# A two-layer diffusion trunk on one core: thirteen inverse square roots, from a VectorE iteration to one GpSimd power each

## The chip, the cores and the metric

The kernel runs on one core of one Trainium2 chip. The metric is the device time of one launch in microseconds (us). Engines are named as the profile names them: PE (TensorE matmuls), PEld (its weight loads), DVE (VectorE), ACT (ScalarE), POOL (GpSimd), SP (SyncE, which issues most DMAs). Each engine works through its own instruction list strictly in order and waits on semaphores for the others.

## The reference, cut to what matters

The reference is one inference step of a trunk of two layers over 384 tokens of width 1024 (128 context tokens and 256 latent tokens). Each layer has an adaLN-modulated RMSNorm, four token mixers that all read the same normed input (A: grouped-query attention, B: gated linear attention, C: differential attention, D: latent attention), gates, an output projection, a second modulated RMSNorm and a gated MLP with a width-3 convolution. One RMSNorm ends the program. What the change touches is the inverse square root in every RMSNorm:

```python
def rmsnorm(x, g):
    xf = x.astype(jnp.float32)
    y = xf * lax.rsqrt(jnp.mean(xf * xf, axis=-1, keepdims=True) + EPS)
    return (y * g.astype(jnp.float32)).astype(x.dtype)

# trunk_layer, twice
h = rmsnorm(x, p['norm1_g']) * (1.0 + sc1) + sh1      # width 1024
aq = rmsnorm(z['a_q'].reshape(...), p['a_qnorm_g'])   # per head, width 64; ak likewise
dq = rmsnorm(z['d_q'], p['d_qnorm_g']) @ p['d_w_uq']  # width 192; d_kv likewise, 128
ob = rmsnorm(ob_raw, p['b_onorm_g']) * silu(...)      # per head, width 64
oc = rmsnorm(oc_raw, p['c_onorm_g']) * (1.0 - lam_init)
h = rmsnorm(x, p['norm2_g']) * (1.0 + sc2) + sh2      # width 1024
```

## The kernel before, in words

Activations for the big projections lie feature-major, in eight tiles of 128 features by 384 tokens. Every fp32 product is made of three fast matmuls: each operand is split into a high and a low part (`wh`, `wl` for weights, `hh`, `hl` for the normed input), and PE does high by high, high by low and low by high. So each weight tile that SP loads (`raw`) passes ACT (a cast to `wh`) and DVE (`wl = raw - wh`) before PE can use it. Matmuls into PSUM banks named `d` are these projections; banks `m` serve the mixers, `x` the sums and broadcasts.

No order is written out by hand. All work is written as streams (Python generators) that yield one instruction, or a short list, at a time. A planner keeps a modelled clock for each engine and always emits next the instruction that could start earliest, then by priority. The order of every engine's list is thus an outcome of the planner's prices. An instruction other than a matmul or a DMA is priced by `price`, and its result counts as ready after the engine's latency in `LAT`, with 130 ns for an engine that `LAT` doesn't list (GpSimd):

```python
LAT = dict(zip("PVS", LATS))                 # LATS = (210.0, 130.0, 210.0)
...
if self.eng == "S":
    return (51 if psum else 93) + 93 * cols + 0.833 * n
...
return (129 if cols and self.fn in ("scalar_tensor_tensor", "tensor_scalar") else 68) + n * (0.521 if fast else 1.042)
```

Thirteen inverse square roots are made. Five belong to the norms of width 1024 and have three columns, one for each 128 tokens: A0 (start of layer 0), F0 (before its MLP), A1, F1 in layer 1, and A2 at the very end. `stats` sums squares with PE, DVE makes the mean (tile `sm`), `tail` calls `rsqrt`, and `bcast` spreads the result over a PSUM tile with three PE matmuls that read `sm` (in the rows: `x<-cs,sm`). In A0 and A2 all later work needs it. At F0, A1 and F1 the first projection of the next stage (`u_units`, matmuls `d<-hh,wh` of 386 columns) runs on the input before its norm, so that PE has work while the norm is made. The other eight, four in each layer, are in the mixers: `headnorm` for A (18 columns), C and B (12 columns each), and six columns in `mixer_d`. There a DVE multiplication uses the result.

Mixer C is the one that takes a way through DRAM: its transposed queries and keys (`m<-cs,zC` on PE) are stored by SP into `dq` and `dk` and read back in another arrangement (`rt<-dk`), and its first scores are the PE matmuls `m<-rt,zC`. In layer 1 as in layer 0, PE has projections and other mixers' work between the two.

Of the kernel before, what the change touches and what calls it, by code (L numbers as in the profile page):

```python
# [11 lines left out]
I32 = mybir.dt.int32  # L12
U8 = mybir.dt.uint8
AF = mybir.ActivationFunctionType
ALU = mybir.AluOpType
# [35 lines left out]
MG = ((0, 2), (0, 3), (0, 4)), MS[:MN[0]], MS[MN[0]:MN[1]], MS[MN[1]:]  # L51
TICK = 3413.0
WIN, THIN = 4500.0, 0.3
RC = (0.6127977038364543, -2.043313830363309, 1.8766171890415242)


TABLES = {AF.Exp: "EX", AF.Tanh: "EXGE", AF.Ln: "LN", AF.Gelu_apprx_tanh: "GE"}
# [198 lines left out]
def trunk_kernel(es, tc, a, o):  # L256
    nc = tc.nc
    sc = Sched()
    V, S, G, PE, SY = (Engine(k, e) for k, e in zip("VSGPD", (nc.vector, nc.scalar, nc.gpsimd, nc.tensor, nc.sync)))
# [14 lines left out]
    cp = es.enter_context(tc.tile_pool(name="cp", bufs=1))  # L274
# [6 lines left out]
    def T(pool, shape, tag, dt=F32):  # L281
        t = pool.tile(shape, dt, tag=tag, name=tag, bufs=1)
        sc.inherit(t.name, before.get(tag))
        before[tag] = t.name
        return t
# [20 lines left out]
    vec = [T(cp, [128, NVEC], f"vec{l}") for l in range(L)]  # L306
    modT = [T(cp, [128, 48, 2], f"mod{l}") for l in range(L)]
    cact = T(cp, [128, 8, 2], "cact")
    T(cp, [128, 40], "pad1")
    T(wk, [128, 56], "pad2")  # L310
    xd = T(dp, [128, 8 * NT], "xd")
    xs = [None] * 8
# [9 lines left out]
    def C(name):  # L322
        return view(cs0, CS0, name) if name in CS0 else view(cst, CST, name)
# [6 lines left out]
    def mul(out, x, y):  # L330
        return V.tensor_tensor(out, x, y, op=ALU.mult)
# [69 lines left out]
        yield S.copy(h, src)  # L401
        yield sub(lo, src, h.bitcast(F32))

    def rsqrt(y, x, t, u):
        def prod():
            if t.free_size() <= 4:
                for i in range(t.free_size()):
                    yield V.scalar_tensor_tensor(t[:, i:i + 1], y[:, i:i + 1], u[:, i:i + 1], y[:, i:i + 1], op0=ALU.mult, op1=ALU.mult)
            else:
                yield mul(t, y, y)  # L410
                yield mul(t, t, u)

        yield V.tensor_scalar(t.bitcast(I32), x.bitcast(I32), 1, None, op0=ALU.logical_shift_right)
        yield V.tensor_scalar(u, x, RC[0], None, op0=ALU.mult)
        yield V.tensor_scalar(y.bitcast(I32), t.bitcast(I32), -1.0, float(0x5F3759DF), op0=ALU.mult, op1=ALU.add)
        yield from prod()
        yield V.scalar_tensor_tensor(t, t, RC[1], t, op0=ALU.add, op1=ALU.mult)
        yield V.tensor_scalar(u, x, -0.5, None, op0=ALU.mult)
        yield V.scalar_tensor_tensor(y, t, RC[2], y, op0=ALU.add, op1=ALU.mult)
        yield from prod()  # L420
        yield V.scalar_tensor_tensor(y, t, 1.5, y, op0=ALU.add, op1=ALU.mult)

    def mod_setup():
        cv = C("cvec").rearrange("p (k m) -> p k m", k=8)
        th = T(wk, [128, 8, 2], "th0")
        cm["cw"] = T(mx, [128, 8, 32], "oc")
        yield V.memset(cm["cw"], 0.0)
        yield S.activation(th, cv, AF.Tanh, scale=0.5)  # L430
        yield V.scalar_tensor_tensor(th, th, 1.0, cv, op0=ALU.add, op1=ALU.mult)
        yield V.tensor_scalar(cact, th, 0.5, None, op0=ALU.mult)
        yield V.tensor_copy(cm["cw"][:, :, 0:2], cact)
# [63 lines left out]
    def bcast(ph, y, want):  # L497
        b = yield X.ask()
        yield [mm(b[:, 128 * t:128 * t + 128], y[:, t:t + 1].to_broadcast([128, 128]), ident, True, True) for t in range(3)]
        cm["b"], cm["bn"] = b, 8 + want  # L500
        done.add(("b", ph))
        if want:
            cm["bs"] = yield TM.ask()
            yield S.copy(cm["bs"], b[:, :NT])
            done.add(("bs", ph))
            b_used()
# [4 lines left out]
            X.release(cm["b"])  # L511

    def tail(ph, sm, want):
        ms, y, t, u = (sm[:, i, 0:3] for i in range(4))
        yield list(rsqrt(y, ms, t, u))
        yield from bcast(ph, y, want)
        SM.release(sm)

    def stats(ph, want):
        sm = yield SM.ask()  # L520
        ms, bank = sm[:, 0, 0:3], X if ph == "A0" else M

        def total(p, x, t, first, last):
            return mm(p[:, 2 * t:2 * t + 2], x[:, 128 * t:128 * t + 128], C("ones")[:, 0:2], first, last)

        def mean(p, rest):
            v = p[:, 0:6].rearrange("p (t m) -> p t m", m=2)[:, :, 0]
            if rest is None:
                return V.tensor_scalar(ms, v, 1.0 / 1024, EPS, op0=ALU.mult, op1=ALU.add)
            return V.scalar_tensor_tensor(ms, v, 1.0 / 1024, rest, op0=ALU.mult, op1=ALU.add)  # L530

        yield has(("sum", ph))
        p = yield bank.ask()
        yield [total(p, sums, t, True, True) for t in range(3)]
        yield mean(p, None)
        if ph != "A0":
            bank.release(p)
            yield has(("sq7", ph))
            p = yield bank.ask()
            yield [total(p, cm["sq7"], t, True, True) for t in range(3)]  # L540
            yield mean(p, ms)
            SQ.release(cm["sq7"])
        bank.release(p)
        yield from tail(ph, sm, want)
# [119 lines left out]
    def headnorm(d, n, gains):  # L664
        g, h = d.shape[1:3]
        sq = yield cm["E"].ask(n=g)
        v = [x[:, :h * n].rearrange("p (h n) -> p h n", h=h) for x in sq]
        for t in range(g):
            yield S.activation(v[t], d[:, t], AF.Square)
        sm = yield SM.ask()  # L670
        ms, y, t_, u = (sm[:, i, 0:g * h] for i in range(4))
        for t in range(g):
            yield V.tensor_reduce(ms[:, h * t:h * t + h], v[t], AX.X, ALU.add)
        cm["E"].release(*sq)
        yield V.tensor_scalar(ms, ms, 1.0 / n, EPS, op0=ALU.mult, op1=ALU.add)
        yield from rsqrt(y, ms, t_, u)
        yield mul(d, d, y.rearrange("p (g h) -> p g h", g=g).unsqueeze(3).to_broadcast([128, g, h, n]))
        SM.release(sm)
        for h0, h1, gain in gains:
            yield mul(d[:, :, h0:h1], d[:, :, h0:h1], gain.unsqueeze(1).unsqueeze(1).to_broadcast([128, g, h1 - h0, n]))  # L680
# [91 lines left out]
    def mixer_a(l, env):  # L772
# [4 lines left out]
        qk = z[:, :, 0:384].rearrange("p t (h d) -> p t h d", h=6)  # L777
        ga = view(gan, GAN, "ga")
        yield from headnorm(qk, 64, ((0, 4, ga[:, 0:64]), (4, 6, ga[:, 64:128])))
        yield G.dma_start(o["ak"][l], z[:, 0, 256:384])  # L780
        yield from rope(qk[:, 1:3], 6, 64, C("cos_a"), C("sin_a"))
# [23 lines left out]
    def mixer_d(l, env):  # L805
# [6 lines left out]
        yield G.dma_start(krc[64:96], a["ckt"][l, 64:96, 512:640])  # L812
        yield G.dma_start(o["kr"][l], z[:, 0, 192:224])
        sm = yield SM.ask()
        ms, y, t_, u = (sm[:, i, 0:6] for i in range(4))
        junk = yield cm["E"].ask()
        for t in range(3):
            yield S.activation(junk[:, :192], z[:, t, 0:192], AF.Square, accum_out=ms[:, t:t + 1])
# [1 line left out]
        cm["E"].release(junk)  # L820
        yield V.tensor_scalar(ms[:, 0:3], ms[:, 0:3], 1.0 / 192, EPS, op0=ALU.mult, op1=ALU.add)
        yield V.tensor_scalar(ms[:, 3:6], ms[:, 3:6], 1.0 / 128, EPS, op0=ALU.mult, op1=ALU.add)
        yield from rsqrt(y, ms, t_, u)
        for t in range(3):
            yield V.scalar_tensor_tensor(z[:, t, 0:192], z[:, t, 0:192], y[:, t:t + 1], view(gan, GAN, "gdq"), op0=ALU.mult, op1=ALU.mult)
            yield V.scalar_tensor_tensor(z[:, t, 224:352], z[:, t, 224:352], y[:, 3 + t:4 + t], view(gan, GAN, "gdk"),
                                         op0=ALU.mult, op1=ALU.mult)
# [69 lines left out]
    def mixer_c(l, env):  # L897
# [137 lines left out]
        for h in range(4):  # L1035
            spawn(head(h), PR["C"], "mx")
        yield has(("oc", l))
        yield from headnorm(oc, 64, ((0, 4, gc),))
        yield has(("bA", l))
        yield from out_T(oc, env, "C")  # L1040
# [4 lines left out]
    def mixer_b(l, env):  # L1045
# [183 lines left out]
        cm["E"].release(*acc)  # L1229
        cm["E"].release(cm["c32"])  # L1230
        yield from headnorm(ob, 64, ((0, 4, view(gan, GAN, "gb")),))
        yield has(("th", l))
        yield mul(ob, ob, th)
# [283 lines left out]
    def begin(env, l):  # L1517
        def late(key, gen):
            yield has(key)
            yield from gen  # L1520

        def fn():
            for nm, z, gen, prio in (("D", "zD", mixer_d, PR["D"]), ("A", "zA", mixer_a, PR["A"]), ("B", "zD", mixer_b, PR["B"]), ("C", "zA", mixer_c, PR["C"])):
                spawn(late((z, l), gen(l, env)), prio, "mx")
            spawn(mods(MG[2 * l], SQ, f"A{l}"), PR["mod"], "md")
            return iter(())

        return fn
# [21 lines left out]
    def startup(env):  # L1550
# [51 lines left out]
        spawn(warm(), 0)  # L1602
        yield SY.dma_start(cs0, a["cs0"])
        spawn(mod_setup(), 0)
        for k in range(8):
            yield SY.dma_start(xtile(k), a["x"][:, NT * k:NT * k + NT])
# [245 lines left out]
```

## Time and profile before

| | us |
|---|---|
| time, median of 3 runs (lowest, highest) | 1363.97 (1362.98, 1369.2) |
| the profiled execution: its time | 1364.65 |
| its span in the profile | 1362.9 |
| PE busy | 1341.4 (98%) |
| DVE busy | 1025.4 (75%) |
| ACT busy | 674.9 (50%) |
| POOL busy | 27.2 (2%) |

The span is the stretch that the profile covers; 1.75 us of the execution's time lie outside it. Matmuls are pipelined, so a busy PE is not PE at its peak, and the TensorE clock that was granted has to be read beside it; its mean over the span is 0.988 of the full 2.4 GHz.

### The profile page before, as it was taken

The numbers are of one execution on the slowest core, as the hardware profiler recorded it, in microseconds if no ns is written. First come the engines' busy times: TensorE is split into PE (matmuls) and PEld (weight loads), VectorE is DVE, ScalarE is ACT, GpSimd is POOL, SyncE is SP. The second block draws the span as 40 slices with busy tenths as digits, with TensorE's granted clock in tenths as the row PEclk, the third lists the DMA queues.
The fourth block names the chain that finished last, engine by engine and source line by source line (L and its number), as shares of the span: only waits on it lengthen the run. The fifth ranks groups of instructions, "written<-read, shape, count | busy, mean of one in ns | idle before, by whom it ended". The sixth has DMA issues, their size and how long they took to land. (4 is left out here: it accounts for less than half of the span.)

```text
span 1362.9 us, 22142 instructions
## 1 busy us (share of the span) xinstructions
PE 1341.4 (98%) x8230; PEld 1239.9 (91%) x8230; DVE 1025.4 (75%) x2141; ACT 674.9 (50%) x1298; POOL 27.2 (2%) x55
## 2 busy tenths in 40 slices
PE   8999999999999999999999999999999999999996
PEld 6786699889999999999998668899999999999996
DVE  5699799876568999997479897786556899655433
ACT  4545665664466444443454666765335564444321
POOL 0000000100000000000001000100000000000000
PEclk8999999999999999999999998999999999999998
DMA  9753675223435666665447445223344365333441
GB/s 357 251 186 117 197 225 154 96 98 108 147 121 183 188 208 202 206 209 180 144 140 246 145 157 168 81 83 107 121 147 136 97 214 180 123 130 118 127 128 60
DMA packets 77084, 214.13 MB, mean 157 GB/s; under 512 B 9616, under 2 KB 17104, under 8 KB 76976
## 3 DMA queue, kind: packets, MB, share of 16 engines
q1 hardware_dynamic: 74592, 206.71, 47.7%
q0 software_dynamic: 2384, 6.00, 1.3%
q8 instruction: 65, 1.06, 0.3%
q14 instruction: 43, 0.35, 0.1%
HBM read 204.78 MB, written 7.90 MB: 156 GB/s over the span
## 5 line engine op out<-in xcount | busy, mean ns | idle before, releaser
L209 ACT CAST wh<-raw 128x1024 fp32r<-128x1024 f32 (+3 forms) x260 | 278.2, 1070 | 264.2 <-PE d L209 175.1
L209 PE MATMUL d<-hh,wl 128*128 128x384 f32 (+1 forms) x1184 | 401.6, 339 | 0.0
L209 PE MATMUL d<-hl,wh 128*128 128x384 f32 (+1 forms) x1184 | 401.4, 339 | 0.0
L209 PE MATMUL d<-hh,wh 128*128 128x384 f32 (+1 forms) x1184 | 399.9, 338 | 0.0
L209 DVE TENSOR_TENSOR wl<-raw,wh 128x1024 fp32r<-128x1024 f32 (+3 forms) x260 | 324.1, 1246 | 94.1 <-ACT wh L209 90.2
L209 PEld LDWEIGHTS d<-hh,wl 128*128 128x128 f32 x1184 | 223.2, 188 | 4.1 <-issue 3.6
L209 PEld LDWEIGHTS d<-hl,wh 128*128 128x128 f32 x1184 | 223.3, 189 | 3.3 <-issue 2.9
L209 PEld LDWEIGHTS d<-hh,wh 128*128 128x128 f32 x1184 | 223.2, 189 | 2.8 <-issue 2.4
L209 PE MATMUL d<-act_l,wh 128*128 128x384 f32 x352 | 117.9, 335 | 0.0
L209 PE MATMUL d<-act_h,wl 128*128 128x384 f32 x352 | 117.8, 335 | 0.0
L209 PE MATMUL d<-act_h,wh 128*128 128x384 f32 x352 | 117.7, 334 | 0.0
L209 DVE SCALAR_TENSOR_TENSOR sq<-sq,cact,sq 128x512 f32<-128x512 f32 x140 | 101.3, 744 | 5.9 <-DMA sq<-wmod_in 5.8
L209 DVE SCALAR_TENSOR_TENSOR mr<-mr,cact,mr 128x512 f32<-128x512 f32 x140 | 100.9, 745 | 0.6 <-DMA mr<-wmod_in 0.4
L209 DVE SCALAR_TENSOR_TENSOR fc<-d,vec,fc 128x255 f32<-128x255 f32 (+1 forms) x152 | 61.6, 412 | 26.1 <-ACT fc L209 25.5
L209 ACT ACTIVATE gt<-d 128x384 f32<-128x384 f32 x64 | 31.3, 490 | 99.5 <-PE d L209 99.4
L209 DVE SCALAR_TENSOR_TENSOR gt<-gt,d 128x384 f32<-128x384 f32 x48 | 26.6, 553 | 69.7 <-PE d L209 62.8
L209 PE MATMUL d<-wh,hh 128*128 128x512 f32 (+2 forms) x192 | 72.0, 375 | 1.3 <-DVE zC L209 1.3
L209 PE MATMUL d<-wh,hl 128*128 128x512 f32 (+2 forms) x192 | 71.0, 370 | 0.0
L209 PE MATMUL d<-wl,hh 128*128 128x512 f32 (+2 forms) x192 | 70.4, 367 | 0.0
L209 PEld LDWEIGHTS d<-act_l,wh 128*128 128x128 f32 x352 | 66.1, 188 | 0.3 <-issue 0.2
L209 PEld LDWEIGHTS d<-act_h,wl 128*128 128x128 f32 x352 | 66.1, 188 | 0.2 <-issue 0.2
L209 PEld LDWEIGHTS d<-act_h,wh 128*128 128x128 f32 x352 | 66.1, 188 | 0.2 <-issue 0.2
(321 smaller groups left out, 2074.7 us busy)
## 6 DMA issues: line engine op xcount, KB each, us to landing
raw<-wgb_in SPq DMA_DIRECT2D x64, 640.0 KB, 3.9
raw<-wf_in SPq DMA_DIRECT2D x72, 512.0 KB, 3.6
sq<-wmod_in SPq DMA_DIRECT2D x80, 256.0 KB, 3.5
mr<-wmod_in SPq DMA_DIRECT2D x80, 256.0 KB, 3.4
raw<-wfd_in SPq DMA_DIRECT2D x32, 448.0 KB, 3.3
raw<-wo_in SPq DMA_DIRECT2D x16, 512.0 KB, 3.6
raw<-wfd_in SPq DMA_DIRECT2D x16, 512.0 KB, 3.5
raw<-wf_in SPq DMA_DIRECT2D x16, 384.0 KB, 3.0
```

The lines of the kernel that those rows point to most:

```text
L209: op.f(*op.args, **op.kw)
```

## The change

`rsqrt` was a first guess from the bits of the number and two correction steps on DVE: 13 instructions for three columns (the two products are then done column by column) and 11 for wider ones. Now it is one `tensor_tensor` of GpSimd with the operation `pow`, whose second operand is a constant tile `half` filled with -0.5 by one DVE memset at the start. The two scratch rows of `sm` are no longer used; the tile keeps its size, and a pad gives up the columns that `half` takes.

```diff
-RC = (0.6127977038364543, -2.043313830363309, 1.8766171890415242)
...
-    T(cp, [128, 40], "pad1")
+    half = T(cp, [128, 24], "half")
+    T(cp, [128, 16], "pad1")
...
-    def rsqrt(y, x, t, u):
-        def prod():
-            if t.free_size() <= 4:
-                for i in range(t.free_size()):
-                    yield V.scalar_tensor_tensor(t[:, i:i + 1], y[:, i:i + 1], u[:, i:i + 1], y[:, i:i + 1], op0=ALU.mult, op1=ALU.mult)
-            else:
-                yield mul(t, y, y)
-                yield mul(t, t, u)
-
-        yield V.tensor_scalar(t.bitcast(I32), x.bitcast(I32), 1, None, op0=ALU.logical_shift_right)
-        yield V.tensor_scalar(u, x, RC[0], None, op0=ALU.mult)
-        yield V.tensor_scalar(y.bitcast(I32), t.bitcast(I32), -1.0, float(0x5F3759DF), op0=ALU.mult, op1=ALU.add)
-        yield from prod()
-        yield V.scalar_tensor_tensor(t, t, RC[1], t, op0=ALU.add, op1=ALU.mult)
-        yield V.tensor_scalar(u, x, -0.5, None, op0=ALU.mult)
-        yield V.scalar_tensor_tensor(y, t, RC[2], y, op0=ALU.add, op1=ALU.mult)
-        yield from prod()
-        yield V.scalar_tensor_tensor(y, t, 1.5, y, op0=ALU.add, op1=ALU.mult)
+    def rsqrt(y, x):
+        yield G.tensor_tensor(y, x, half[:, :x.free_size()], op=ALU.pow)
...
+        yield V.memset(half, -0.5)
...
-        ms, y, t, u = (sm[:, i, 0:3] for i in range(4))
-        yield list(rsqrt(y, ms, t, u))
+        ms, y = (sm[:, i, 0:3] for i in range(2))
+        yield list(rsqrt(y, ms))
...
-        yield from rsqrt(y, ms, t_, u)
+        yield from rsqrt(y, ms)
```

The planner prices the power like a small DVE operation, so the lists of the engines come out in another order, from the first norm on through both layers' mixers. Three places show it. In the rows, the word after the line number is the operation, then the tile written, the tiles read, and the shape.

First, PE at F0, from the last sum of squares (`m<-cs,sq`) to the broadcast. Before:

```order
L209 MATMUL m_4395<-cs_88,sq_4386 128x2 x3
L209 MATMUL d_4374<-hl_75,wh_4288 128x386
L209 MATMUL d_4375<-hh_74,wh_4288 128x386
L209 MATMUL d_4375<-hh_74,wl_4289 128x386
L209 MATMUL d_4375<-hl_75,wh_4288 128x386
...
L209 MATMUL d_4375<-hh_80,wh_4330 128x386
L209 MATMUL d_4375<-hh_80,wl_4331 128x386
L209 MATMUL x_4425<-cs_88,sm_4372 128x128 x3
L209 MATMUL d_4375<-hl_81,wh_4330 128x386
```

Of the change:

```order
L208 MATMUL m_4345<-cs_88,sq_4336 128x2 x3
L208 MATMUL d_4324<-hl_75,wh_4238 128x386
L208 MATMUL d_4325<-hh_74,wh_4238 128x386
L208 MATMUL d_4325<-hh_74,wl_4239 128x386
L208 MATMUL d_4325<-hl_75,wh_4238 128x386
L208 MATMUL x_4363<-cs_88,sm_4322 128x128 x3
L208 MATMUL d_4324<-hh_76,wh_4238 128x386
```

The broadcast stood behind 21 projection matmuls and stands behind 4 now. The counts are the same at A1 and F1.

Second, the start (A0), on PE and on DVE. `m<-cs,ms` is the step that makes the first modulation columns, which DVE then finishes as `mod`. PE before:

```order
L209 MATMUL x_211<-cs_88,sums 128x2 x3
L209 MATMUL m_178<-rt_166,oc 32x256 x4
L209 MATMUL m_178<-cs_88,ms_224 128x2 x2
L209 MATMUL x_241<-cs_88,sm_176 128x128 x3
L209 MATMUL m_249<-s_185,oc 32x256 x4
```

PE of the change:

```order
L208 MATMUL x_213<-cs_88,sums 128x2 x3
L208 MATMUL m_180<-rt_168,oc 32x256 x4
L208 MATMUL x_231<-cs_88,sm_178 128x128 x3
L208 MATMUL m_180<-cs_88,ms_226 128x2 x2
L208 MATMUL m_242<-s_187,oc 32x256 x4
```

The broadcast has changed places with the modulation step. DVE of the change, from the mean on:

```order
L208 TENSOR_SCALAR sm_178<-x_213 128x3
L208 TENSOR_TENSOR mod_94<-m_180,vec_92 128x2 x2
L208 TENSOR_TENSOR wl_188<-raw_179,wh_186 128x896
L208 SCALAR_TENSOR_TENSOR mod_94<-mod_94,vec_92 128x2
L208 SCALAR_TENSOR_TENSOR sq_250<-xs_125,mod_94,x_231 128x128
```

Before, the same four rows stood behind the mean in the same order, with the 13 instructions of `rsqrt` between the mean and them.

Third, POOL at the start, of the change. `ISA` is an instruction that the build puts ahead of the first power (the library that GpSimd is to use); no such row stood there before.

```order
L208 ISA
L208 TENSOR_TENSOR sm_178<-sm_178,half 128x3
L208 DMA kT_662<-ckt_in 128x128
L208 DMA pk<-pkd_in 128x1280
```

The power comes ahead of POOL's first DMA, and the others likewise take their places between its DMAs. On PE in layer 1, 67 matmuls stood between the last transpose of C's keys (`m<-cs,zC`) and C's first score (`m<-rt,zC`), 26 of them projections of 512 columns and 5 of 384; 98 stand there now, 33 of 512 and 38 of 384. In layer 0 it was 80 (27 and 12) and is 76 (54 and 4).

## Rows read from the trace of the kernel before

**Rows 1.** The page's first part: busy time, share of the span, instructions.

```profile
PE 1341.4 (98%) x8230; PEld 1239.9 (91%) x8230; DVE 1025.4 (75%) x2141; ACT 674.9 (50%) x1298; POOL 27.2 (2%) x55
```

**Rows 2.** Waits of PE: who for whom, total us, times, longest.

```profile
PE m L209 <- DMA rt<-dk: 2.9, 2, 2.3
...
PE m L209 <- DVE am L209: 1.6, 2, 0.9
```

**Rows 3.** Timeline of PE, C in layer 1: start, length, instruction, idle before.

```profile
809.42 0.49 PE L209 MATMUL m<-cs,zC 128*128 128x128 f32 x3
...
822.40 0.33 PE L209 MATMUL d<-hh,wh 128*128 128x384 f32 x1
822.58 0.34 PE L209 MATMUL d<-hh,wl 128*128 128x384 f32 x1
825.26 0.70 PE L209 MATMUL m<-rt,zC 96*128 96x128 f32 x3 [2.34 <-DMA rt<-dk]
...
828.19 0.52 PE L209 MATMUL d<-hh,wh 128*128 128x384 f32 x1
828.51 0.52 PE L209 MATMUL d<-hh,wl 128*128 128x384 f32 x1
```

**Rows 4.** Stretches of 2 us: busy time by engine, then PEclk, DMA share, GB/s.

```profile
826.00:828.00 2.00, 2.00 (x6) 0.96 (x5) 1.50 (x3) 0.19 (x1) 0.00 (x0) 0.54 0.46 112
...
836.00:838.00 2.00, 2.00 (x12) 2.00 (x11) 0.87 (x5) 1.53 (x4) 0.00 (x0) 0.90 0.46 156
```

**Rows 5.** Tile sm: instructions that write it; ns minimum/median/maximum.

```profile
L209 DVE SCALAR_TENSOR_TENSOR sm<-sm x69: 155/171/221, 14.2 to 1353.8; 128x1 f32<-128x1 f32 x30, 128x3 f32<-128x3 f32 x15, 128x12 f32<-128x12 f32 x12, 128x18 f32<-128x18 f32 x6
```

**Rows 6.** Timeline of POOL, first rows.

```profile
0.35 0.10 POOL L1838 MEMSET const-uint8-127<- 128x1 uint8 x1
...
49.82 0.54 POOL L209 DMA_DIRECT2D pk<-pkd_in  x1 [47.88 <-PE m L209]
```

**Rows 7.** Timeline of the start (A0).

```profile
13.46 1.08 PE L209 MATMUL m<-rt,oc 128*32 128x256 f32 x8
13.57 0.16 DVE L209 TENSOR_SCALAR sm<-x 128x3 f32<-128x3 f32 x1 [2.78 <-PE x L209]
...
15.04 1.01 PE L209 MATMUL m<-cs,ms 128*128 128x2 f32 x4 [0.49 <-ACT ms L209]
...
15.91 1.63 PE L209 MATMUL x<-cs,sm 128*128 128x128 f32 x6
16.14 0.23 DVE L209 TENSOR_TENSOR mod<-m,vec 128x2 f32<-128x2 f32 x2 [0.38 <-PE m L209]
16.28 1.09 DVE L209 TENSOR_TENSOR wl<-raw,wh 128x896 fp32r<-128x896 f32 x1
17.29 0.15 DVE L209 SCALAR_TENSOR_TENSOR mod<-mod,vec 128x2 f32<-128x2 f32 x1
...
17.57 0.74 DVE L209 SCALAR_TENSOR_TENSOR sq<-xs,mod,x 128x128 f32<-128x128 f32 x2
...
19.33 0.80 PE L209 MATMUL d<-wh,hh 128*128 128x512 f32 x1
```

**Rows 8.** Timeline of the end (A2).

```profile
1351.76 0.16 DVE L209 SCALAR_TENSOR_TENSOR sm<-m,sm 128x3 f32<-128x3 f32 x1 [1.41 <-PE m L209]
...
1354.01 1.65 PE L209 MATMUL x<-cs,sm 128*128 128x128 f32 x6 [2.28 <-DVE sm L209]
```

**Rows 9.** Timeline at F0, PE and DVE.

```profile
407.96 0.42 PE L209 MATMUL d<-hl,wh 128*128 128x386 f32 x1
408.14 0.16 DVE L209 SCALAR_TENSOR_TENSOR sm<-m,sm 128x3 f32<-128x3 f32 x1 [0.74 <-PE m L209]
...
410.25 0.56 DVE L209 TENSOR_TENSOR hl<-sq,hh 128x386 fp32r<-128x386 f32 x1
...
411.75 0.83 PE L209 MATMUL x<-cs,sm 128*128 128x128 f32 x6
```

**Rows 10.** Timeline of PE, C's first score in layer 0.

```profile
165.15 0.70 PE L209 MATMUL m<-rt,zC 96*128 96x128 f32 x3 [0.52 <-DMA rt<-dk]
```

More of the change, by code (lines that the diff above doesn't have):

```diff
@@ L670, in headnorm @@
         sm = yield SM.ask()
-        ms, y, t_, u = (sm[:, i, 0:g * h] for i in range(4))
+        ms, y = (sm[:, i, 0:g * h] for i in range(2))
         for t in range(g):
@@ L814, in mixer_d @@
         sm = yield SM.ask()
-        ms, y, t_, u = (sm[:, i, 0:6] for i in range(4))
+        ms, y = (sm[:, i, 0:6] for i in range(2))
         junk = yield cm["E"].ask()
@@ L822, in mixer_d @@
         yield V.tensor_scalar(ms[:, 3:6], ms[:, 3:6], 1.0 / 128, EPS, op0=ALU.mult, op1=ALU.add)
-        yield from rsqrt(y, ms, t_, u)
+        yield from rsqrt(y, ms)
         for t in range(3):
```

## The prediction

> **What bounds the kernel now.** I read the busy times first, then PE's waits, then the timeline where a wait stood. PE is busy for 1341.4 us of the 1362.9 us span, DVE for 75% [rows 1]. So time is won or lost where PE stands still, and DVE's load by itself decides nothing. The list of PE's waits is short. Between the start and the end it holds two kinds that matter: the first scores of mixer C waiting for `dk` to come back from DRAM, 2.9 us in two waits, and the attention statistics, 0.9 us at the longest [rows 2].
>
> One of these waits costs more than its length. In layer 1 PE stands still for 2.34 us before C's first score [rows 3]. Right after it the granted clock is 0.54 in the stretch from 826 us, and 0.90 in the one from 836 us, that is, half of full speed (1.2 instead of 2.4 GHz) for about 10 us between [rows 4]. The reader sees what that does in the spacing of two equal matmuls: 0.18 us before the wait (822.40 and 822.58), 0.32 us after it (828.19 and 828.51) [rows 3]. 10 us at that pace do 10 x 0.18 / 0.32 = 5.6 us of work, so about 4.4 us are lost on top of the 2.34. The waits of up to 0.9 us [rows 2] are not followed by a lower clock: outside the start and end, the clock is below full speed only here.
>
> **What leaves DVE.** Five norms lose 13 instructions each and eight lose 11, 153 in all. At 0.171 us, the median of their largest group [rows 5], that is 26 us of DVE time for 13 powers on POOL, which is busy for 2% [rows 1]. I count this at nothing: DVE has a quarter of its time free, and PE does not wait for it except at the places below. What counts is how long the way from the mean to its user takes, and where the planner now puts that user.
>
> **The price of a power.** The trace has no GpSimd arithmetic. Its cheapest POOL instruction is a memset of one column, 0.10 us, its dearest kind a DMA issue of 0.54 us [rows 6]. From below I take one memset, 0.1 us. From above, a power as a program of as many steps as the 13 instructions that it replaces, each at the DMA issue's price: 7.0 us. Thirteen steps at the memset's price give 1.3 us. I take this one, because the memset is the only POOL row that computes in SBUF as the power does. Call it X, counted from the end of the mean to the start of the broadcast, so hand-overs are in it.
>
> **The start (A0).** Before: the mean ends at 13.73, the broadcast runs from 15.91 to 17.54, and the first scaled input starts on DVE at 17.57 [rows 7]. Now PE has the broadcast ahead of the modulation step, and DVE has the modulation, the weight split (1.09 us) and the modulation's scaling ahead of the scaled input. So what used to run beside the inverse square root runs behind it. With X = 1.3 the broadcast starts at 15.03 (PE is free from 14.54, when `m<-rt` ends), ends 1.63 later at 16.66; the modulation step takes 1.01 (17.67), its DVE addition 0.23 (17.90), the split 1.09 (18.99), the scaling 0.15 (19.14) [rows 7]. The scaled input starts at 19.14 instead of 17.57: 1.6 us later, and PE's first projection, 19.33 before, with it. Even with X = 0.1 it is 14.54 + 1.63 + 1.01 + 0.23 + 1.09 + 0.15 = 18.65, 1.1 us late; beyond 0.8 us each us of X is one more. PE is loaded from then on, so I carry all of it: **+1.6**.
>
> **The end (A2).** Nothing covers it. The mean ends at 1351.92 and the broadcast starts at 1354.01 [rows 8]: 2.09 us, now X. **-0.8**.
>
> **F0, A1 and F1.** Here the iteration was covered. At F0 the mean ends at 408.30 and the broadcast started only at 411.75, when PE came to it [rows 9]. The planner believes in a fifth of a microsecond for the power and puts the broadcast behind 4 matmuls instead of 21. Those 4 start at 407.96 [rows 9] and at 0.18 us each [rows 3] are over at 408.68, which covers 0.38 us. PE then stands still for 1.3 - 0.38 = 0.92 us, in the middle of work that it could have done. The same order holds at A1 and F1: 3 x 0.92 = **+2.8**. Below X = 0.38 it is nothing. 0.92 us is about the longest wait that left the clock alone [rows 2].
>
> A row speaks for a longer way here: behind the mean, DVE's list now has the split `hl<-sq,hh`, 0.56 us [rows 9], which reads two SBUF tiles, where before it had `rsqrt`. If the two engines run side by side, nothing changes. The Trainium skill, "SBUF — State Buffer", section "Who interferes with whom", says that a DVE instruction with two SBUF inputs and a GpSimd one share a port pair, and the later one waits for the whole of the other. No GpSimd operation of this trace shows it; by that rule each of the three places would wait up to 0.56 us more, 1.7 us in all.
>
> **Mixer C.** The power itself shortens A's and D's norms, and the whole order of the mixers shifts. In layer 1 there are now 98 PE matmuls instead of 67 between C's last key transpose and its first score. The 31 more are almost all projections; 7 more of 512 columns (0.18 x 512 / 384 = 0.24 us each) and 33 more of 384 (0.18) come to 7.6 us, less some 1.5 us for the small mixer matmuls that have left. PE took from 809.91 to 822.92 for the 67, and `dk` was there at 825.26 [rows 3]; with 6 us more to do it arrives after the data. I count the wait and the slow clock as gone: -2.3 - 4.4 = **-6.7**. In layer 0 the 76 matmuls hold 27 more of 512 columns and 8 fewer of 384 than the 80 did, so the 0.52 us [rows 10] should go as well: **-0.5**. Against it: SP issues the loads in its own new order, with two `wgb` loads ahead of the second `dk` store in layer 1, and each waits for a weight buffer. This is the term I trust least.
>
> **The mixers' own norms.** The DVE multiplication now stands 0 to 4 instructions behind its mean, and DVE waits there up to X instead of working 11 x 0.17 = 1.9 us. With X near 1.3 to 2 for the wider ones that is even: 0. DMAs of POOL behind a power wait for it too; they are stores and early loads that nobody is waiting for at that time.
>
> **The sum.** 1.6 - 0.8 + 2.8 - 6.7 - 0.5 = -3.6 us. Against the profiled execution's own 1364.65 us that is 1361.0; the median of the runs shown is 0.7 lower than that execution, within what they scatter. I forecast **1361.0**.
>
> **Rivals.**
> *The wait in C stays*, or an equal one appears in the new order (waits on SP's queue speak for it, the larger filling against it): 1361.0 + 6.7 = 1367.7.
> *A slow power* (the other side). If X is 2.7 us, the start loses 3.0, the end 0.6, and F0, A1 and F1 stand still for 2.32 us each, 7.0. That is the length of the wait after which the clock fell [rows 3, 4], so 4.4 us of slow clock follow each, 13.2. With C's gain, 3.0 + 0.6 + 7.0 + 13.2 - 7.2 = +16.6: 1381. It decides from X somewhere between 1.3 (0.92 us of waiting, clock kept) and 2.7. For it speaks that a power is no simple step; against it, only three columns.
> *A nearly free power*: X = 0.1 gives +1.1 - 2.0 + 0 - 7.2 = -8.1, 1356.6.
> *A late first power.* The `ISA` row ahead of it has no row before to be priced by. It has from the program's start to 13.73 [rows 7] for nothing; each us beyond is a us at the start, and it takes 9.8 us beyond before the total passes 1370.8. The Trainium skill, "GPSIMD Engine Reference", section 2.1, says that the first call of freshly loaded GpSimd code pays about 6 us; if that came behind the wait, an estimate by that page is 1367, and if it runs during the wait, nothing changes.
>
> **How the numbers follow.** The sum's case 0.45, C's wait stays 0.20, slow power 0.16, late first power 0.10, nearly free 0.09. 0.5% of the time, 6.8 us, is about what a measurement of this kernel can tell from no change: 1357.2 and 1370.8. Faster: the nearly free power and 0.06 of the sum's case, 0.15. Slower: the slow power, 0.03 of the late one, 0.05 of C's (with some waiting more), 0.24. The rest, 0.61, is the same. The sum's case alone reaches from 1357 to 1365. The range reaches from just below the nearly free power to just short of the slow one's price, 1355 to 1379.
>
> **What would show it.** In the changed profile: POOL `sm` rows of about 1.3 us; PE waiting for POOL about 0.9 us before `x<-cs,sm` near 408, 692 and 1074 us, with the clock kept; PE's first `d` matmul near 20.9 us; the broadcast at the end 1.3 us behind the mean; no wait of PE for `rt<-dk` near 825 us and no clock below full there. The prediction is wrong if those three waits exceed 2 us, if the clock falls behind them, or if a wait of mixer C survives.

## The result, and the profile after

Slower by 1.0%: 1377.59 us (median of 5 runs, 1377.02 to 1381.62) against 1363.97 for the kernel before (median of 5 runs, 1359.29 to 1369.83), a ratio of 1.0102 with a 95% interval of 1.0071 to 1.0133. The forecast was 1361.0, no change; the time lies at the upper end of its range (1355 to 1379), and on the other side of before. The profiled execution took 1381.62 us with a span of 1379.8, 4 us above the median; its span is 16.9 us longer than that of before.

The first part of the page of the changed kernel, to read against [rows 1], and the groups of POOL that read `half`, that is, the powers (busy us, mean ns of one | idle time before, releaser):

```profile
PE 1350.0 (98%) x8230; PEld 1244.8 (90%) x8230; DVE 1007.5 (73%) x1989; ACT 674.6 (49%) x1298; POOL 51.2 (4%) x68
```

```profile
L208 POOL TENSOR_TENSOR sm<-sm,half 128x12 f32<-128x12 f32 x4 | 9.5, 2381 | 206.2 <-DVE sm L208 206.2
L208 POOL TENSOR_TENSOR sm<-sm,half 128x18 f32<-128x18 f32 x2 | 6.9, 3430 | 7.7 <-DVE sm L208 7.7
L208 POOL TENSOR_TENSOR sm<-sm,half 128x3 f32<-128x3 f32 x5 | 4.6, 927 | 522.8 <-DVE sm L208 522.8
...
L208 POOL TENSOR_TENSOR sm<-sm,half 128x6 f32<-128x6 f32 x2 | 2.7, 1366 | 1.6 <-DVE sm L208 1.6
```

DVE lost 152 instructions and 17.9 us of busy time (the prediction had 26), and that gained nothing. The powers are not one price: 0.93 us for 3 columns, 1.37 for 6, 2.38 for 12, 3.43 for 18. The prediction had 1.3 us, and 1.3 to 2 for the wider ones.

The waits of PE of the changed kernel (who for whom, total us, times, longest), to read against [rows 2]:

```profile
PE m L208 <- DMA rt<-dk: 3.5, 1, 3.5
PE x L208 <- POOL sm L208: 3.1, 5, 1.2
PE d L208 <- DVE zC L208: 2.1, 1, 2.1
PE m L208 <- DVE zA L208: 2.1, 2, 1.7
PE m L208 <- DVE oc L208: 1.5, 2, 1.2
PE m L208 <- DVE k L208: 1.3, 1, 1.3
```

PE waits for POOL itself only 3.1 us. The new names are DVE's: `zA`, `oc` and `k` are what DVE multiplies by the mixers' inverse square roots. The wait for `zC` is mostly not the powers': 1.7 us of it stay in e3 below, where no power runs. DVE in turn waits 11.3 us for POOL, all of it at these multiplications:

```profile
DVE k L208 <- POOL sm L208: 4.9, 2, 2.5
DVE oc L208 <- POOL sm L208: 3.1, 2, 2.2
DVE zA L208 <- POOL sm L208: 3.0, 2, 2.7
DVE zD L208 <- POOL sm L208: 0.3, 1, 0.3
```

Where the 16.9 us came in can be read at the broadcasts (`x<-cs,sm`), which mark the same point of the work in both. At F0 it starts at 426.95 instead of 411.75 with 17 matmuls less ahead of it (17 x 0.18 = 3.1 us), so the changed kernel is 18.3 us late there. At A1 it is 712.19 - 695.51 + 3.1 = 19.8, at F1 1092.11 - 1077.28 + 3.1 = 17.9, and at A2 1370.91 - 1354.01 = 16.9. So nearly all of it comes in layer 0 before its MLP; from F0 to A1 it is 1.5 more, layer 1's mixers give 1.9 back, the end 1.0. The starts before:

```profile
695.51 0.83 PE L209 MATMUL x<-cs,sm 128*128 128x128 f32 x6
...
1077.28 0.83 PE L209 MATMUL x<-cs,sm 128*128 128x128 f32 x6
```

From 20 us up to F0, PE's waits sum to 9.0 us in six (2.14, 0.24, 3.50, 1.20, 1.31, 0.62) against 2.1 in three, and the clock accounts for the rest. The stretches of 20 us of that part in which it was below 0.95 (busy time by engine, PEclk, DMA share, GB/s):

```profile
20.00:40.00 20.00, 19.89 (x118) 13.25 (x120) 10.43 (x30) 6.28 (x13) 0.00 (x0) 0.85 0.90 325
80.00:100.00 20.00, 17.86 (x112) 13.87 (x113) 17.28 (x47) 11.25 (x33) 0.54 (x1) 0.91 0.37 112
160.00:180.00 20.00, 16.50 (x70) 13.51 (x69) 13.20 (x23) 11.22 (x22) 0.00 (x0) 0.83 0.88 257
240.00:260.00 20.00, 20.00 (x130) 17.36 (x128) 14.48 (x32) 11.38 (x27) 0.00 (x0) 0.83 0.29 99
```

Before, the first of them had 0.98 and the others 1.00. The missing parts are 20 x (0.15 + 0.09 + 0.17 + 0.17) = 11.6 us, so 6.9 us more waiting and about 11 of slow clock make the 18 in this execution. The slow clock is not the same in every execution: the mean clock of this one is 0.983, that of the three which took 1377.0 to 1377.6 us is 0.988, as in the profiled execution before. So the 4 us by which this execution lies above the median are likely slow clock of its own, and the median has less than 11.

### The profile page after: what moved, and what is told of

The parts are those of the page before. It is cut to its first block, busy times and chain, and to the rows that moved or that the text cites. A ratio compares the mean times of both kernels' runs of the same rounds, so it can differ in the third digit from the quotient of the medians.

```text
span 1379.8 us, 22044 instructions
## 1 busy us (share of the span) xinstructions
PE 1350.0 (98%) x8230; PEld 1244.8 (90%) x8230; DVE 1007.5 (73%) x1989; ACT 674.6 (49%) x1298; POOL 51.2 (4%) x68
## 4 chain that ended last, share of the span: by engine, by line
PE 87%; DVE 6%; DMA 3%; POOL 1%; issue 1%; ACT 1%; SPq 1%; POOLq 0%; DVEq 0%; ACTq 0%
PE d L208 70%; PE m L208 15%; DVE sq L208 2%; PE x L208 1%; POOL sm L208 1%; DMA dk<-rt 1%; DVE wl L208 1%; SPq L208 1%; DVE e L208 0%; DVE sm L208 0%; DMA rt<-dk 0%; DVE zA L208 0%; DMA pk<-wmp_in 0%; DVE zD L208 0%; ACT e L208 0%
## 5 line engine op out<-in xcount | busy, mean ns | idle before, releaser
L208 PE MATMUL d<-wh,hl 128*128 128x512 f32 (+2 forms) x192 | 74.1, 386 | 0.0
```

The source lines that it names most:

```text
L208: op.f(*op.args, **op.kw)
```

## The experiments

Ratios are to the kernel before, run beside each on the same chip. Theory W: the cost is the length of the powers, which engines wait for, DVE in the mixers above all. Theory O: the cost is the new order of the lists, whatever the power takes.

**Half of the change each (e1, e2).** The other norms keep the old iteration, under the name `iterate`.

```diff
# e1: mixers          # e2: stats
-yield from rsqrt(y, ms)
+yield from iterate(y, ms, t_, u)
...
-yield list(rsqrt(y, ms))
+yield list(iterate(y, ms, t, u))
```

> Power only in the five norms of width 1024 (three columns); the eight norms in the mixers keep the VectorE iteration. Theory W (the wide powers in the mixers cost the time, because VectorE stands behind them): what is left is 0.6 + 0.5 + 0.6 us of PE waiting at F0, A1 and F1, about 0.9 later at the start and 1.0 gained at the end, so about 1365, between 1361 and 1369. Theory O (the new order of the engines' lists costs the time, whatever made it): part of the order changes here too, so somewhere between the two kernels, 1368 to 1376.

> Power only in the eight norms in the mixers; the five of width 1024 keep the iteration. Theory W: nearly all of the loss is here, 1374 to 1380. Theory O: between the two kernels, 1368 to 1376, and about as much as with the five alone.

Measured: e1 1363.53 us, 1.0007 (0.9987 to 1.0027); e2 1378.49, 1.0115 (1.0086 to 1.0144). Against the iteration, five powers of three columns cost nothing on balance; the eight in the mixers cost the whole loss. Both are new orders too, so this alone does not exclude theory O.

**The same lists, another length (e3).**

```diff
-yield V.memset(half, -0.5)
+yield V.memset(half, 0.05)
...
-yield G.tensor_tensor(y, x, half[:, :x.free_size()], op=ALU.pow)
+yield G.tensor_tensor(y, x, half[:, :x.free_size()], op=ALU.mult)
```

> The GpSimd operation is a multiplication by 0.05 in place of the power, so the norms are not normed; every engine's list is the one of the changed kernel, row for row, and only the length of the 13 GpSimd operations differs. Theory W: with 0.1 to 0.3 us each the waits behind POOL go and the time falls to 1358 to 1366. Theory O: the lists are the same, so the time stays at 1372 to 1378.

Measured: 1364.91 us, 1.0014 (0.9993 to 1.0035; the kernel before had 1363.74 beside it). With the lists of the changed kernel, row for row, 12.7 of the 13.6 us go when the 13 operations are short. Theory W holds in sum. Not everything went, though: in e3 as in the changed kernel PE waits 3.5 us for C's keys in layer 0, and this part belongs to the order.

The small sum hides two large parts of the order that nearly cancel. The broadcasts of e3 at F0 and F1:

```profile
419.09 0.93 PE L208 MATMUL x<-cs,sm 128*128 128x128 f32 x6
...
1078.66 0.93 PE L208 MATMUL x<-cs,sm 128*128 128x128 f32 x6
```

Counted as above, in us behind the kernel before:

| | F0 | A1 | F1 | A2 |
|---|---|---|---|---|
| changed kernel | 18.3 | 19.8 | 17.9 | 16.9 |
| e3, the same lists | 10.4 | 11.3 | 4.5 | 2.8 |

So the lists alone lose 10.4 us in layer 0 before its MLP and win 6.8 back in layer 1's mixers; the length of the powers adds 7.9 and 5.0 there. These are single executions, but e5 below, with powers only in the five norms of width 1024, has 10.4 at F0 and 4.6 at F1 as well.

**The same lists, the power in some places only (e5, e6, e7).** The others multiply. e5 has one more memset, since its powers are real.

```diff
-op=ALU.pow
+op=ALU.pow if x.free_size() in (18, 6) else ALU.mult   # e6; (12,) in e7, (3,) in e5
```

> The lists of the changed kernel, row for row, but for one more memset at the start; real powers in the five norms of width 1024 only, a multiplication by 0.05 in the other eight (not normed). Theory W: of the 12.7 us between the powers and the multiplications (1377.6 against 1364.9) the five account for the small part, that is 0.6 us more waiting of PE at each of F0, A1, F1 and A2 and about 0.7 at the start, 3.1 in all: 1366 to 1370. Theory P (each power costs alike, 12.7 / 13 = 1 us): 1370.

> The lists of the changed kernel, row for row; a power (with the exponent 0.05) only in the norms of A and D (18 and 6 columns), a multiplication in the other nine. Theory W: mostly layer 1, where PE waits 1.7 us behind them and the clock falls after it; 4 to 5 us over the multiplications, 1368 to 1371. Theory P: 4 us, 1369. The two agree here; the run is for the sum of the three parts, which by theory W is 12.7 us if the parts add up.

> The lists of the changed kernel, row for row; a power (with the exponent 0.05) only in the norms of C and B (12 columns), a multiplication in the other nine. Theory W: four waits of DVE of 2.2 to 2.5 us, of which PE sees 1.2 and 1.3 in layer 0 and 0.3 in layer 1, and slow clock behind the first; 4 to 6 us over the multiplications, 1369 to 1371.

Measured: e5 1369.31 us, 1.0039 (1.0020 to 1.0059); e6 1368.00, 1.0034 (1.0019 to 1.0050); e7 1369.29, 1.0044 (1.0025 to 1.0062). Above e3 that is 4.4, 3.1 and 4.4 us, in sum 11.9 of 12.7: the parts add up. But they do not follow the widths. That five narrow powers account for the small part was wrong; about 1 us for each of the 13 fits as well, within what these runs can tell. The waits say why: a narrow one is waited for by PE at once, a wide one by DVE, and PE sees what is left of it (DVE's waits for POOL: 0.8 us in e3 and e5, 4.1 in e6, 8.0 in e7). In e5 PE waits 0.66, 0.47, 0.66 and 1.25 us for POOL; in e7 1.24 and 1.30 us in layer 0 for `oc` and `k`.

**The powers run, nobody waits (e13).** Open was whether the engines lose by waiting or by running beside GpSimd.

```diff
-    def rsqrt(y, x):
-        yield G.tensor_tensor(y, x, half[:, :x.free_size()], op=ALU.pow)
+    def rsqrt(y, x, t):
+        yield G.tensor_tensor(y, x, half[:, :x.free_size()], op=ALU.mult)
+        nc.gpsimd.tensor_tensor(t, x, half[:, :x.free_size()], op=ALU.pow)
```

> The lists of the changed kernel, but each GpSimd operation is a multiplication by 0.05 that the consumers wait for, and behind it on POOL stands a power of the same width (exponent 0.05) into a scratch row that nobody reads; nothing is normed. Theory W (waiting): the powers run but no engine waits for them, so the time is that of the multiplications alone, 1363 to 1367. Theory C (contention: VectorE is slowed while GpSimd computes): a good part of the 12.7 us comes back, 1370 to 1378.

Measured: 1370.90 us, 1.0049 (1.0029 to 1.0069), where the waiting theory had 1363 to 1367. The trace shows why: at the five norms of width 1024, whose instructions are made as one list, the scratch power was issued ahead of the multiplication, so those five were waited for after all. In the mixers the waits did go: DVE waits 1.2 us for POOL in all, where it was 11.3. The wait of PE in e13:

```profile
PE x L208 <- POOL sm L208: 4.0, 5, 1.4
```

In e3 it was 0.6 us, once. So e13 is to be held against e5, in which the same five are waited for: 1.6 us more, inside what the two intervals leave open. Taken by themselves, those intervals would let contention in the mixers cost up to some 5 us (an estimate from their widths). The traces leave it little: the broadcast at the end starts 4.0 us later than in e3, 3.4 of which are the additional waits at the five places, and 14.1 us later in the changed kernel. And DVE instructions that run within a power keep their length (0.74 and 1.22 us in the rows of e4 below).

**The true price (e4).** The planner gets the price that the trace of the changed kernel shows.

```diff
+        if self.eng == "G" and self.fn == "tensor_tensor":
+            return 330.0 + 172.0 * n
         fast = self.fn in ("tensor_copy", "tensor_scalar") and not psum
```

> All 13 powers, but the planner now prices a GpSimd tensor_tensor as the trace shows it, 330 ns and 172 ns for each column (0.85 us for 3, 2.4 for 12, 3.4 for 18). Theory W: VectorE no longer stands behind the power and PE's broadcasts stand later; 1360 to 1368. Theory O: another order again, which may cost as much as the first, 1364 to 1380, and no reason to end below before.

Measured: 1357.92 us, 0.9963 (0.9945 to 0.9981), the best of all kernels here, 19.7 us below the changed one. The powers are as long as before, but something else stands behind them. Layer 1, A's norm, DVE and POOL, in the changed kernel (start, length, instruction, idle before):

```profile
751.35 0.17 DVE L208 TENSOR_SCALAR sm<-sm 128x18 f32<-128x18 f32 x1
751.43 0.74 DVE L208 SCALAR_TENSOR_TENSOR sq<-sq,cact,sq 128x512 f32<-128x512 f32 x1
...
751.68 3.61 POOL L208 TENSOR_TENSOR sm<-sm,half 128x18 f32<-128x18 f32 x1 [2.29 <-DVE sm L208]
...
752.48 0.17 DVE L208 TENSOR_SCALAR sm<-sm 128x3 f32<-128x3 f32 x1 [0.31 <-ACT e L208]
...
755.32 1.36 DVE L208 TENSOR_TENSOR zA<-zA,sm 128x1152 f32<-128x1152 f32 x1 [2.67 <-POOL sm L208]
```

DVE has done all that its list holds ahead of the multiplication (`zA<-zA,sm`) by 752.65, and stands still for 2.67 us. PE gets the result of the chain behind it for the transposes of `zA` (`m<-cs,zA`) too late, and after that the clock is at half for some 4 us (PE's timeline, then stretches of 2 us). These two waits of PE are there in e6 too, with the powers of A and D alone, and in none of e3, e5, e7 and e13:

```profile
763.50 0.33 PE L208 MATMUL m<-cs,zA 128*128 128x128 f32 x1 [0.39 <-DVE zA L208]
765.53 0.33 PE L208 MATMUL m<-cs,zA 128*128 128x128 f32 x1 [1.71 <-DVE zA L208]
```

```profile
764.00:766.00 2.00, 0.47 (x3) 0.41 (x4) 1.97 (x7) 0.11 (x1) 0.00 (x0) 1.00 0.52 184
766.00:768.00 2.00, 2.00 (x11) 1.68 (x10) 2.00 (x5) 1.24 (x4) 0.00 (x0) 0.65 0.27 33
768.00:770.00 2.00, 2.00 (x7) 1.25 (x6) 0.97 (x4) 1.47 (x2) 0.00 (x0) 0.50 0.86 256
770.00:772.00 2.00, 2.00 (x9) 1.29 (x9) 1.63 (x5) 0.81 (x4) 0.00 (x0) 1.00 0.61 236
```

The same place in e4:

```profile
734.29 0.74 DVE L210 SCALAR_TENSOR_TENSOR sq<-sq,cact,sq 128x512 f32<-128x512 f32 x1
...
734.54 5.34 POOL L210 TENSOR_TENSOR sm<-sm,half 128x18 f32<-128x18 f32 x2 [2.29 <-DVE sm L210]
...
735.42 0.74 DVE L210 SCALAR_TENSOR_TENSOR sq<-sq,cact,sq 128x512 f32<-128x512 f32 x1
...
736.15 1.41 DVE L210 SCALAR_TENSOR_TENSOR sq<-sq,cact,sq 128x512 f32<-128x512 f32 x2
...
737.48 1.22 DVE L210 TENSOR_TENSOR wl<-raw,wh 128x1024 fp32r<-128x1024 f32 x1
...
738.61 0.75 DVE L210 SCALAR_TENSOR_TENSOR sq<-sq,cact,sq 128x512 f32<-128x512 f32 x1
...
739.27 1.35 DVE L210 TENSOR_TENSOR zA<-zA,sm 128x1152 f32<-128x1152 f32 x1
```

The 5.34 us are the two powers of A and D one behind the other. DVE has five sums and a weight split to do meanwhile, and the multiplication follows them without a wait; PE's two waits at `m<-cs,zA` are gone. In all of e4, DVE waits for POOL nowhere.

**How much is the draw of the order (e8, e9, e10, e11, e12, e14, e15)?** Every kernel above but e3, e5, e6, e7 and e13 is also another order. The one number that the planner has for the latency of a VectorE result was moved, in the kernel before, the changed one and the one with the true price. No instruction changes. In e15 the price of the power is 0.5 us higher.

```diff
-LATS = (210.0, 130.0, 210.0)
+LATS = (210.0, 150.0, 210.0)     # e8, e12, e14; 110.0 in e9, e10, e11
...
-            return 330.0 + 172.0 * n
+            return 830.0 + 172.0 * n     # e15
```

> The kernel before, with its 153 instructions of the iteration, but the planner counts a VectorE result as ready after 150 ns and not 130. Nothing but the order of the lists changes. It measures what another order is worth by itself: theory W says that orders alone move the time by a few us (1360 to 1370) and so cannot be told from the 5.8 us that the true price gained; a rival says that the gain of the true price comes from the power itself, and then this one is within 2 us of 1364.

> The kernel before with a VectorE latency of 110 ns in the planner: a third draw of the order for the iteration (1364 with 130, 1374 with 150). Theory D (the time of any of these kernels is its order's draw, some 10 us wide, and the power adds to it only what it makes engines wait for): anywhere from 1358 to 1376. Theory K (130 is simply the right latency): 1366 to 1376.

> The changed kernel (power priced at 0.07 to 0.09 us) with a VectorE latency of 110 ns in the planner. Theory W (the unpriced power costs some 13 us of waiting on top of whatever order): 1370 to 1388, and above the kernel with the iteration at the same latency. Theory D alone (the loss was one bad draw): as often below as above it.

> All powers at their true price, VectorE latency 110 ns in the planner. Theory W: the waits behind POOL stay away in any order, so below the changed kernel at the same latency by about 10 us or more; against the iteration at the same latency theory T (the power is worth it by itself) says lower by 3 to 8 us, theory D says either sign.

> All powers at their true price, VectorE latency 150 ns. Theory T: below the iteration at the same latency (1374.1) by 3 us or more. Theory D: a draw of its own, 1356 to 1376. Theory W: no waits for POOL beyond the two of the start and the end in either case.

> The changed kernel with its own low price, VectorE latency 150 ns in the planner; the third pair. Theory W: some 10 to 16 us above the kernel with the true price at the same latency (1358.8), 1368 to 1378. Theory D (draws of the order): below 1368 is as likely.

> The true price and 0.5 us more for each power, for what a VectorE operation under way adds to it. If the true price still leaves waits (two on PE, and VectorE behind some powers), this removes them: 1354 to 1358. Theory D: another draw, 1356 to 1372.

Measured, each as median and ratio to the kernel before (interval):

| latency in the planner | iteration | power, low price | power, true price |
|---|---|---|---|
| 110 | 1361.93, 1.0007 (0.9988 to 1.0026) | 1374.34, 1.0098 (1.0076 to 1.0119) | 1360.97, 1.0001 (0.9985 to 1.0016) |
| 130 | the kernel before | 1377.59, 1.0102 (1.0071 to 1.0133) | 1357.92, 0.9963 (0.9945 to 0.9981) |
| 150 | 1374.10, 1.0074 (1.0050 to 1.0098) | 1377.42, 1.0099 (1.0066 to 1.0132) | 1358.83, 0.9980 (0.9962 to 0.9997) |

The iteration itself moves by 0.7% with its order, so a single order proves little. The low price is 1% above the kernel before in all three orders, and the true price 13 to 20 us below it in all three, so that loss is no draw. DVE's waits for POOL say the same: 11.7, 11.3 and 13.0 us with the low price, none in any of the three kernels with the true one. Against the iteration at the same latency the low price loses 12.4, 13.6 and 3.3 us, and the true price is equal once and below it twice, by 0.4% and 0.9%; three draws do not settle how large that gain is. e15 came to 1361.27, 0.9987 (0.9964 to 1.0011), not to 1354 to 1358: with the true price there was no wait left behind the powers in the mixers that 0.5 us more could have removed. The 3.3 us above e4 are of the size that other orders made.

## Why the prediction was wrong

**Two steps failed, about equally.** The forecast was 3.6 us below the kernel before, the result 13.6 above: 17.2 apart. For a nearly free operation the prediction's sum was -8.1; e3, with these lists and operations of 0.2 to 0.6 us, came to +0.9. So 9.0 of the 17.2 lie in what the prediction made of the lists, and there in layer 0: up to F0 its terms gave 1.1 - 0.5 = 0.6, and e3 is 10.4 late. The other 8.2 lie in the power's length, for which it had 4.5 (from -8.1 to -3.6) and which cost 12.7. That the time still fell inside the range is luck: the range reached so far up only for "A slow power".

**The length: "The mixers' own norms", 0.** It took X, a price fitted to three columns, for norms of 6, 12 and 18, with "1.3 to 2 for the wider ones", and weighed DVE's wait against the DVE instructions saved. Both were wrong. The power takes 0.17 us for each column (0.85 to 3.43 from 3 to 18, a slope of 2.58 / 15), and DVE's time was never what was short: I had said so myself under "What leaves DVE", and then let it pay for a wait. What counts is that PE needs the result of the multiplication next. With the lists held, e6 and e7 put 7.5 us on these eight, where the term had 0.

**The lists: "In layer 0 ... the 0.52 us should go as well", -0.5.** It went to 3.5. I counted PE's matmuls between the last transpose and the first score, and not the way of the data. C's way in layer 0 of the changed kernel (SP's stores and loads, ACT's cast, PE):

```profile
145.55 0.86 SPq L208 DMA_DIRECT2D dk<-rt  x2
...
151.56 0.27 ACT L208 CAST rt<-m 128x128 fp32r<-128x128 f32 x1 [0.65 <-DMA dk<-rt]
```

```profile
156.41 0.86 SPq L208 DMA_DIRECT2D dk<-rt  x2
...
161.57 0.33 SPq L208 DMA_DIRECT2D rt<-dk  x1
```

```profile
170.10 1.19 PE L208 MATMUL m<-rt,zC 96*128 96x128 f32 x3 [3.50 <-DMA rt<-dk]
```

ACT casts the second half of the keys into `rt` only when the first store from it has landed, the second store goes out 10.9 us after the first (some 4 of them behind the cast, with weight loads ahead of it in SP's list), and the loads 5.2 us behind that. From the last key transposes (147.46) to the score that is 22.6 us, where before it was 18.1 (147.01 to 165.15 [rows 10]). It stays 3.54 us in e3, so it is the order and no power that makes this wait. Its length differs between executions of these same lists: 1.17 us in e7, 1.82 in e5, 2.28 in e6, 2.98 in e13. In the changed kernel the clock stood at 0.50 from 170 to 176 us behind it; it fell to half in e3, e6 and e13 too, and stayed full in e5 and e7. The rest of e3's 10.4 us is the wait for `zC` (1.72 instead of 0.65) and the clock from 20 to 28 us and near 250, for which the prediction had no term. In layer 1 the same count came out right: **-6.7** stands (in e3 layer 1's mixers win 6.8), the wait is 0.60 us instead of 2.34, and the clock behind it is full. It survived as a wait, though, which the prediction had named as a sign against itself, and the clock did fall later, to 0.50 from 876 us:

```profile
857.45 0.70 PE L208 MATMUL m<-rt,zC 96*128 96x128 f32 x3 [0.60 <-DMA kT<-dk]
```

```profile
858.00:860.00 2.00, 2.00 (x13) 2.00 (x13) 1.19 (x4) 1.93 (x6) 0.00 (x0) 1.00 0.70 169
```

**F0, A1 and F1: +2.8.** Right in place and kind, and 1.7 in size (0.62, 0.47, 0.62): the broadcast stands behind four matmuls, PE waits, the clock stays full. F0, to read against [rows 9]:

```profile
425.56 0.16 DVE L208 SCALAR_TENSOR_TENSOR sm<-m,sm 128x3 f32<-128x3 f32 x1 [0.74 <-PE m L208]
425.64 0.55 DVE L208 TENSOR_TENSOR hl<-sq,hh 128x386 fp32r<-128x386 f32 x1
...
425.87 1.03 POOL L208 TENSOR_TENSOR sm<-sm,half 128x3 f32<-128x3 f32 x1 [100.59 <-DVE sm L208]
...
426.95 0.93 PE L208 MATMUL x<-cs,sm 128*128 128x128 f32 x6 [0.62 <-POOL sm L208]
```

**The end: -0.8.** Measured -1.0: the mean ends at 1369.86 and the broadcast starts at 1370.91, 1.05 us instead of 2.09 [rows 8]. X for three columns was a fair guess.

**The start: +1.6.** From the end of the mean (12.51) to the first scaled input (17.23) it is 4.72 us, where it was 3.84 [rows 7]: +0.9, with 0.99 for X. The mean came 1.2 us earlier, so PE's first projection started at 18.08 and not later, as I had said, but the clock came back from half at about 26 us and not at 21, which the term did not have. In e1, e4, e5 and e12, too, the mean clock of the stretch from 20 to 40 us is 0.82 to 0.86 (and 0.87 in e8, with the iteration; 1.00 in e2 and e9).

**The rivals.** "A slow power" had 1381 and was near in number, but not in mechanism: it had narrow powers of 2.7 us with the clock falling at F0, A1 and F1, and neither came. "A late first power" is out: the first one starts 0.08 us behind the mean and takes 0.85 us, as long as the last, 1357 us later. The Trainium skill, "GPSIMD Engine Reference", section 2.1, has about 6 us for the first call of freshly loaded code. No run here shows them: POOL stood idle for 12.15 us ahead of this power, so that they either ran in that time, which is the prediction's other case, or were not paid. "The wait in C stays", or an equal one appears, came true in layer 0 (3.50 us, and about 6 at half clock behind it); its 1367.7 lacks the length of the powers. No rival named the wide powers.

## What to carry to other kernels

An operation that moves to an engine for which no row exists has to be priced for each width that occurs, at the lowest and the highest, before anything is concluded from one; here the narrow case was right, and the wide one cost most of what the length cost. Where a planner sets the order, its price for the new operation is part of the change: with the price wrong, consumers were put straight behind a power of 3.4 us, and with it right neither DVE nor PE waited for that power. A change that reorders the lists has two effects, and a run with the same lists and a short operation tells them apart: here the order lost 10.4 us in one layer and won 6.8 in the other, which no total shows. And before a gain of half a percent is believed, the same kernel should be run in a few other orders, since those alone moved this one by 0.7%.

## What the runs showed of the hardware

**The power's price.** On GpSimd a power of 128 rows takes 0.85 us for 3 columns and 0.16 to 0.17 more for each further one (18 columns alone in e13: 3.25); a multiplication of the same shapes takes 0.19 to 0.22 us from 3 to 18 columns (e3, where no DVE instruction as below is in its way). So it is the power, not the engine, that is dear.

**GpSimd behind a DVE instruction, not the other way round.** A multiplication of 12 columns in e3 that started while DVE ran an instruction with several SBUF inputs (POOL and DVE):

```profile
229.95 0.74 DVE L208 SCALAR_TENSOR_TENSOR sq<-sq,cact,sq 128x512 f32<-128x512 f32 x1
...
230.19 0.58 POOL L208 TENSOR_TENSOR sm<-sm,half 128x12 f32<-128x12 f32 x1 [97.51 <-DVE sm L208]
```

Its like without such a neighbour took 0.20 to 0.21; this one ended 0.08 us behind DVE's. The powers at F0 and F1 that started within `hl<-sq,hh` took 1.03 us. At A1 the power started first, at 711.26, and the split 0.24 us into it: the power took 0.87, and the split 0.56, as before [rows 9]; the five DVE instructions within the two powers of e4 above kept their lengths too. The Trainium skill, "SBUF — State Buffer", section "Who interferes with whom", has a lock on a shared port pair by which the later of the two waits. The trace agrees where GpSimd is the later one, by 0.16 to 0.4 us here and by 1.3 to 1.5 at A's norm in layer 1 of e2 (18 columns in 4.75 us), where two such DVE instructions follow each other; it does not where DVE is the later one.

**The clock fell without a wait.** In the changed kernel PE had no gap from 248 to 258 us, but from 248.14 to 252.50 it ran little else than 24 matmuls of `m<-s` on 32 rows. PE's timeline, and two stretches behind it:

```profile
249.26 1.26 PE L208 MATMUL m<-s 32*128 32x128 f32 x12
...
251.00 1.50 PE L208 MATMUL m<-s 32*128 32x128 f32 x6
```

```profile
252.00:254.00 2.00, 2.00 (x8) 1.78 (x7) 0.02 (x1) 1.41 (x4) 0.00 (x0) 0.50 0.43 172
...
258.00:260.00 2.00, 2.00 (x22) 1.71 (x20) 0.48 (x1) 1.71 (x5) 0.00 (x0) 1.00 0.00 0
```

The clock was at half to 258 us, which is the slow stretch at 240 us above. It is 1.00 there in the kernel before, with the same products further apart (253.14 to 259.72), and 0.91 in e3. The packing alone is not the cause: e13 ran the same sequence from 246.33 to 250.12, and e12 its 24 from 247.19 to 249.99, and in both the clock was 1.00 from 240 to 260. In e3, e5, e6 and e7, with the same lists, it fell. What decides is open.
